# Top-k selection by seven interpolated counts with a branch to a bit search, and the adaLN weight sums on VectorE

## The chip, the cores and the metric

The kernel runs on one core of a Trainium2 chip. A NeuronCore has a matmul engine (TensorE, "PE" in the profile, with its weight loads as "PEld"), and VectorE ("DVE"), ScalarE ("ACT"), GpSimd ("POOL") and SyncE ("SP", which issues the DMAs). Each engine works through its own instructions in order and waits on semaphores for the others. The metric is the device time of one execution in microseconds; the median of several runs is given.

## The reference

A trunk of two layers over 1024 positions and 1024 channels. Each layer modulates its normalised input (adaLN), projects it once, and runs a gated MLP over chunks beside a sparse attention. The attention scores all keys with a small indexer and keeps, for each query, the 256 best:

```python
logits = jnp.einsum('bthd,bsd->bths', qib, k_idx) * (IDX_DIM ** -0.5)
score = jnp.einsum('bth,bths->bts', wb, jax.nn.relu(logits)).astype(jnp.float32)
score = jnp.where(causal[None], score, -jnp.inf)
_, idx = lax.top_k(score, top)                      # top = 256
valid = idx <= qpos[None, :, None]
k_sel, v_sel = gather(k, idx), gather(v, idx)
sc = jnp.einsum('bthd,btkd->bthk', qb, k_sel).astype(jnp.float32) * attn_scale
p = jax.nn.softmax(jnp.where(valid[:, :, None, :], sc, -jnp.inf), axis=-1)
return jnp.einsum('bthk,btkd->bthd', p, v_sel)
```

adaLN: `mod = silu(c) @ w_ada + b_ada`, cut into shift, scale and gate; `h = layer_norm(x) * (1 + scale) + shift`; at the end `x = layer_norm(ALPHA * x + gate * (y @ w_out))`.

## The kernel before

Queries are handled in eight blocks of 128 rows, one query per partition. Block i sees (i + 1) x 128 keys, so blocks 0 and 1 keep every key and only blocks 2 to 7 need a selection. Nothing is gathered: the kernel computes dense attention and adds a mask of 0 or -3e38, so the selection has to deliver, for each row, which 256 keys stay.

A layer (`layer`, L871) goes through these stages:

1. keys, values and indexer queries are projected, then `scores` (L496) builds a float32 tile `sc2` to `sc7` of 128 x (i + 1) x 128 per block: TensorE makes the logits of a head, ScalarE applies the relu, VectorE multiplies by the head's weight and adds up (L513).
2. the remaining input projections (`specs`, L878 to L884): v, q, u, z_a, z_b, two weight slices each, four accumulations of 24 matmuls (L326) into a PSUM accumulator `acc`, of which there are two. `u_za` takes the u accumulations off on VectorE (L469) and the z_a ones on ScalarE and GpSimd (L472, L473); `zb` uses ScalarE alone. The spatial gating (`sgu`, L445) lies between. Between the yields of these projections `side` (L905) advances two kinds of generators: the searches in `gens`, all of them at each step, and the adaLN weight sums in `back`, from the sixth weight slice on. So selection and adaLN sums lie beside the projections in each engine's queue; a scheduler in the compiler then orders each engine's instructions by its own estimate, within stretches that a branch ends.
3. attention per block and half of the heads (`att_soft`, L660, and `att_pv`, L686), interleaved with the output projection (L735), its weights being loaded and multiplied by the gate first (`load_wout`, L710).

The search before is exact, in three groups of blocks (`GROUPS`, L53): blocks 7, 6 and 5 search the 256th largest score bit by bit, the count of each of 31 bits being made on ScalarE (L544) with decisions on VectorE (L545, L553); blocks 4 and 3 search 16-bit keys in two times 16 counts on VectorE (L574, L583, L585); block 2 searches 31 bits with float32 counts on VectorE (L519, L552, L553). A count is one VectorE pass that compares a whole tile with a threshold per row and adds up the hits:

```python
self.nc.vector.tensor_scalar(j[:, :n], sc, thr, None, op0=op, op1=ALU.add, accum_out=out)
```

At the start of attention `select_mask` (L636) turns each tile into its mask: a count, an equality pass, a scan (L647) to cut ties, two more passes (L648, L649) and a GpSimd pass (L650).

`ada_sum` (L166) adds up `w_ada` rows weighted by the condition, over eight slices of 128 x 1024 per sum, three sums in layer 0 (its own gate, and shift and scale of layer 1) and one in layer 1. `ADAE` (L64) chooses the engine: 0 is GpSimd, a multiply (L182) and an add (L184) per slice.

## Time and profile before

| what | us |
|---|---|
| median of 3 runs | 1233.45 (1232.51 to 1239.79) |
| the profiled execution | 1233.29 |
| its span, first to last instruction | 1231.5 |
| TensorE busy | 1119.0 |
| VectorE busy | 977.5 |
| ScalarE busy | 707.1 |
| GpSimd busy | 706.5 |

The profile is of one execution. "Busy" counts an engine's own instructions, not its waits. A view by stretches gives each engine's busy time between two moments of the span; the view in order of time gives start and length of single instructions, and a length can reach into the next instruction, so the distance from start to start is what an instruction costs its engine's queue. A count is followed by a short instruction that reads the accumulator (DVE_READ_ACCUMULATOR).

### The profile page before, as it was taken

To read this page: it belongs to the slowest core of one execution; us is meant where nothing else is said; L and a number is where in the kernel's file an instruction comes from. 1 tells how busy PE (TensorE), PEld (TensorE's weight loads), DVE (VectorE), ACT (ScalarE), POOL (GpSimd) and SP (SyncE) were. 2 spreads that over 40 slices of the span, in tenths; PEclk is the share of its full clock that TensorE was granted. 3 is DMA by queue.
4 is the path that set the end of the run, shared out by engine and by line. 5 is a ranking of instruction groups with operands and counts; after the bars stand their busy time and mean duration, and the time that the engine had idled before them with its cause. 6 is when DMAs were issued, how large, how long until landed. Compare 5 with 4: busy or idle time off the path is not lost.

```text
span 1231.5 us, 18024 instructions
## 1 busy us (share of the span) xinstructions
PE 1119.0 (91%) x5456; PEld 887.3 (72%) x5456; DVE 977.5 (79%) x2776; ACT 707.1 (57%) x1344; POOL 706.5 (57%) x556
## 2 busy tenths in 40 slices
PE   5989999897999499989989999999899967999997
PEld 1568888766788388766667788877678856777885
DVE  6784767998989965788976467599999898878775
ACT  0342655778794164565765345557789535667561
POOL 1574314997794785564765531189633378555753
PEclk9899999998999799999999999999999988999999
DMA  8936332347454474331322463144431434333311
GB/s 257 275 104 165 104 86 79 136 138 222 140 170 154 142 222 125 103 112 44 94 86 69 120 172 86 52 163 137 147 125 52 141 100 142 83 104 86 112 35 60
DMA packets 126777, 152.15 MB, mean 124 GB/s; under 512 B 17108, under 2 KB 94292, under 8 KB 126680
## 3 DMA queue, kind: packets, MB, share of 16 engines
q1 hardware_dynamic: 126680, 151.01, 40.3%
q8 instruction: 43, 0.70, 0.2%
q14 instruction: 54, 0.44, 0.1%
HBM read 111.38 MB, written 35.40 MB: 119 GB/s over the span
## 4 chain that ended last, share of the span: by engine, by line
PE 49%; DVE 30%; issue 7%; ACT 6%; DMA 6%; SPq 2%; POOL 0%; DVEq 0%; ACTq 0%; POOLq 0%
PE pacc L326 18%; PE pacc L735 13%; DVE junkd L574 4%; PE ps L673 4%; PE ppt L693 4%; DVE junkd L519 3%; PE ppt L506 3%; ACT junka L544 3%; PE po L699 2%; PE po L698 2%; PE ps L506 2%; DMA h<-in_w_ada 1%; DVE gb L647 1%; DVE bn L211 1%; DVE bi L553 1%
## 5 line engine op out<-in xcount | busy, mean ns | idle before, releaser
L326 PE MATMUL pacc<-h,w 128*128 128x512 f32 (+2 forms) x2304 | 550.0, 393 | 13.0 <-ACT gc L472 4.8
L326 PEld LDWEIGHTS pacc<-h,w 128*128 128x128 f32 (+1 forms) x2304 | 423.6, 189 | 111.2 <-ACT gc L472 6.4
L280 POOL TENSOR_TENSOR w<-wr,w 128x512 fp32r<-128x512 f32 (+1 forms) x100 | 131.6, 1334 | 168.4 <-ACT w L279 161.2
L544 ACT ACTIVATE junka<-sc,bi 128x1024 int8<-128x1024 f32 x186 | 193.5, 1040 | 51.0 <-DVE bi L553 23.4
L735 PE MATMUL pacc<-h,gc 128*128 128x512 f32 x768 | 196.5, 400 | 2.9 <-ACT gc L279 2.5
L735 PEld LDWEIGHTS pacc<-h,gc 128*128 128x128 f32 x768 | 142.6, 191 | 31.8 <-ACT gc L279 3.2
L513 DVE SCALAR_TENSOR_TENSOR sc<-gc,wi,sc 128x384 f32<-128x384 f32 (+3 forms) x140 | 101.8, 768 | 52.6 <-ACT gc L508 50.1
L673 PE MATMUL ps<-kd,q 128*128 128x512 f32 (+4 forms) x384 | 106.2, 376 | 31.5 <-DVE mx L674 24.8
L697 DVE TENSOR_TENSOR ga<-ppt,ga 128x512 fp32r<-128x512 f32 x144 | 96.6, 684 | 18.1 <-ACT ga L696 17.2
L696 ACT ACTIVATE ga<-ppt 128x512 fp32r<-128x512 f32 x144 | 82.7, 593 | 34.8 <-PE ppt L693 33.6
L574 DVE TENSOR_SCALAR_CACHE_REDUCE junkd<-r,cnt 128x640 bf16<-128x640 int16 (+3 forms) x128 | 102.5, 801 | 0.1
L673 PEld LDWEIGHTS ps<-kd,q 128*128 128x128 f32 x384 | 65.6, 198 | 49.5 <-DVE mx L674 37.1
L682 POOL TENSOR_SCALAR w<-w,rd 128x256 f32<-128x256 f32 (+6 forms) x77 | 62.5, 815 | 42.5 <-DVE rd L681 22.7
L679 ACT ACTIVATE w<-w,mx 128x256 f32<-128x256 f32 (+6 forms) x77 | 60.7, 788 | 42.6 <-DVE mx L674 42.0
L279 ACT ACTIVATE w<-wr 128x512 fp32r<-128x512 f32 (+1 forms) x100 | 56.0, 598 | 44.1 <-DMA wr<-in_w_in 22.0
L693 PE MATMUL ppt<-ident,w 128*128 128x128 f32 x349 | 75.5, 277 | 0.3 <-ACT gc L256 0.3
L216 POOL TENSOR_TENSOR rs<-rs,mhalf 128x1 f32<-128x1 f32 x48 | 32.1, 676 | 73.1 <-DVE rs L215 73.0
L693 PE MATMUL ppt<-ident,ya 128*128 128x128 f32 x227 | 59.1, 277 | 15.4 <-DVE modT L192 15.4
L698 PE MATMUL po<-ga,vv 128*128 128x512 f32 x144 | 62.1, 431 | 9.4 <-DVE gb L705 6.4
L508 ACT ACTIVATE gc<-ppt 128x384 f32<-128x384 f32 (+3 forms) x96 | 47.9, 525 | 36.9 <-PE ppt L506 31.5
L184 POOL TENSOR_TENSOR r<-r,r 128x1024 f32<-128x1024 f32 x28 | 68.2, 2437 | 0.1
L345 POOL TENSOR_TENSOR ga<-ga,ga 128x512 fp32r<-128x512 f32 (+2 forms) x40 | 48.4, 1215 | 33.5 <-ACT ga L344 29.2
(202 smaller groups left out, 2109.4 us busy)
## 6 DMA issues: line engine op xcount, KB each, us to landing
wr<-in_w_in SPq DMA_DIRECT2D x50, 512.0 KB, 4.2
r<-in_w_ada SPq DMA_DIRECT2D x32, 512.0 KB, 4.3
q<-q SPq DMA_DIRECT2D x112, 128.0 KB, 3.0
q<-ga SPq DMA_DIRECT2D x48, 256.0 KB, 2.2
h<-in_w_ada SPq DMA_DIRECT2D x32, 256.0 KB, 5.4
wr<-in_w_out SPq DMA_DIRECT2D x16, 512.0 KB, 4.0
r<-r SPq DMA_DIRECT2D x14, 512.0 KB, 3.4
r<-x SPq DMA_DIRECT2D x12, 512.0 KB, 4.2
```

Of the source, the lines that this page charges most:

```text
L184: eng.tensor_tensor(acc, acc, w, op=ALU.add)
L280: self.nc.gpsimd.tensor_tensor(lo, src, hi.bitcast(F32), op=ALU.subtract)
L326: self.nc.tensor.matmul(acc[:m, :tn], w[:, k, :m], h[:, k % 2, t0:t0 + tn], start=(k == 0 and i == 0), stop=(k == NK - 1 and i == 2))
L513: nc.vector.scalar_tensor_tensor(sc[:, c0:c0 + w], r[:, :w], wsc, sc[:, c0:c0 + w], op0=ALU.mult, op1=ALU.add)
L544: nc.scalar.activation(j[:, :ns[c]], scs[c], AF.Sign, bias=thr, accum_out=cnt[:, c:c + 1])
L574: self.nc.vector.tensor_scalar(j[:, :keys.shape[1]], keys, thr, None, op0=ALU.is_ge, op1=ALU.add, accum_out=out)
L673: nc.tensor.matmul(ps[:, :w], q[:, g * 4 + h, :], self.KD[x][:, c0:c0 + w], start=(x == 0), stop=(x == 1))
L693: nc.tensor.transpose(pt[:, h * P:(h + 1) * P], pr[h][:, kt * P:(kt + 1) * P], self.ident)
L696: nc.scalar.activation(ph, pt, AF.Copy)
L697: nc.vector.tensor_tensor(pl, pt, ph.bitcast(F32), op=ALU.subtract)
L698: nc.tensor.matmul(o, self.V[:, kt, :], ph, start=(kt == 0), stop=False)
L735: self.nc.tensor.matmul(acc, s[:, k, :], m[:, cs], start=(first and k == i == 0), stop=(not more and k == 3 and i == 2))
```

## The change

The selection is rebuilt. Six blocks form two groups, 2 to 4 and 5 to 7. For each row a first threshold comes from mean and variance of its first 256 scores and a table (`start_table`), with a guessed bracket around it. Seven times the threshold is counted; the bracket's lower end (count at least 256) or upper end (count below 256) is replaced by it, and the next threshold is interpolated between the ends for a count of 252. The counts run on VectorE, the arithmetic between them on GpSimd, on 128 x 3 to 128 x 12 elements. A row is left over when the upper end's count is below 248 after seven steps. TensorE adds up the rows left over, VectorE reads the sum into a register, and where it isn't zero a branch runs `exact` for the three blocks of the group: a float32 bit search of 31 bits on VectorE, with scans for ties. Behind the branch each block gets its mask: the keys above the upper end stay, and of the others the up to eight largest are taken with a max-8 and a match-and-replace. All of it now lies beside the projections, and attention starts with finished masks. `side` advances one search per step, in turn, where it advanced all.

With `ADAE = (1, 1, 1)` all adaLN sums run on VectorE, one instruction per slice (a scaled add) instead of GpSimd's two.

The diff, cut to its core:

```diff
-    GROUPS = ((0, 7, 6, 5), (16, 4, 3), (32, 2))
-    MLEAD = 16
+    GROUPS = ((2, 3, 4), (5, 6, 7))
+    STEPS = 7
-    ADAE = (0, 0, 0)
+    ADAE = (1, 1, 1)
...
+    def select(self, masks, blocks, grp):
...
+        yield
+        for k in range(self.STEPS):
+            for c, i in enumerate(blocks):
+                self.count(masks[i], (i + 1) * P, V[:, 0, c:c + 1], ALU.is_ge, C[:, c:c + 1])
+            pool.tensor_scalar(V[:, 1, :], C, 1.0, -float(MID), op0=ALU.mult, op1=ALU.add)
+            pool.tensor_scalar(M[:, 0, :, :], rep(C, 2), float(TOP), 1.0, op0=ALU.is_lt, op1=ALU.mult)
+            pool.tensor_scalar(M[:, 1, :, :], rep(C, 2), float(TOP), 1.0, op0=ALU.is_ge, op1=ALU.mult)
+            pool.tensor_scalar(M[:, 2, :, :], rep(C, 2), float(TOP), 1.0, op0=ALU.is_lt, op1=ALU.mult)
+            pool.tensor_tensor(pair(Z), pair(Z), M[:, 0:2].rearrange("p h k g -> p h (k g)"), op=ALU.mult)
...
+            pool.tensor_tensor(Z, Z, U, op=ALU.add)
...
+            elif k + 1 < self.STEPS:
+                pool.tensor_tensor(W, Z[:, 0:2, :], Z[:, 2:4, :], op=ALU.subtract)
+                pool.tensor_tensor(R, W[:, 1, :], self.minus6[:, :G], op=ALU.pow)
+                pool.tensor_tensor(R, R, W[:, 0, :], op=ALU.mult)
+                pool.tensor_tensor(R, R, Z[:, 1, :], op=ALU.mult)
+                pool.tensor_tensor(V[:, 0, :], Z[:, 0, :], R, op=ALU.subtract)
+            yield
+        bad = small("sb", 1)[:, 0, :]
+        pool.tensor_scalar(bad, Z[:, 3, :], float(TOP - 8 - MID), 1.0, op0=ALU.is_lt, op1=ALU.mult)
+        pt = self.p("pt")
         for c in range(G):
+            nc.tensor.matmul(pt[0:1, 0:1], bad[:, c:c + 1], self.ones[:, 0:1], start=(c == 0), stop=(c + 1 == G))
         yield
+        flag = self.t(f"flag{grp}", [1, 1], I32)
+        nc.vector.tensor_copy(flag, pt[0:1, 0:1])
+        yield
+        v = nc.vector.value_load(flag[0:1, 0:1])
+        with self.tc.If(v != 0):
+            for c, i in enumerate(blocks):
+                self.exact(masks[i], (i + 1) * P)
+                nc.vector.memset(Z[:, 2, c:c + 1], 1.5)
+                nc.vector.memset(Z[:, 3, c:c + 1], float(TOP - 8 - MID))
...
+        for c, i in enumerate(blocks):
+            sc, n = masks[i], (i + 1) * P
+            w = self.g("gb", [P, SEQ], BF16)
+            nc.vector.tensor_scalar(w[:, :n], sc, Z[:, 2, c:c + 1], -2.0 * LOW, op0=ALU.is_lt, op1=ALU.mult)
+            nc.vector.scalar_tensor_tensor(sc, w[:, :n], LOW, sc, op0=ALU.add, op1=ALU.min)
+            yield
+            m8 = self.t("m8", [P, 8], bufs=2)
+            nc.vector.max(m8, sc)
+            nc.vector.tensor_tensor(m8, m8, Q[:, c, :], op=ALU.min)
+            yield
+            nc.vector.match_replace(sc, m8, sc, LOW)
+            nc.vector.tensor_scalar(sc, sc, LOW, NEG, op0=ALU.not_equal, op1=ALU.mult)
+            yield
+
+    def exact(self, sc, n):
...
         for b in range(30, -1, -1):
...
+            cnt, dec, f2 = self.cnt_tile(), self.int_tile(), self.int_tile()
+            self.count(sc, n, f[:, 0:1].bitcast(F32), ALU.is_ge, cnt)
+            nc.vector.tensor_scalar(dec, cnt, float(TOP), float(1 << b), op0=ALU.is_lt, op1=ALU.mult)
+            nc.vector.tensor_scalar(f2, dec, f[:, 0:1], (1 << b) >> 1, op0=ALU.bitwise_xor, op1=ALU.bitwise_xor)
             f = f2
...
-                for g in gens:
-                    next(g, None)
+                while gens and next(gens[0], 0) == 0:
+                    gens.pop(0)
+                gens.append(gens.pop(0)) if gens else None
...
-            for i in order:
-                if i > 1 and t == max(2 * order.index(i) - self.MLEAD, -1):
-                    self.select_mask(masks[i], i)
```

How the order moves, in layer 0. First VectorE, before, where the third u accumulation of the second slice is taken off (`ya` times `pacc`, L469); `junkd` and `cnt` are a count, `bi` the bits of a threshold:

```order
L585 TENSOR_SCALAR cnt_3247<-cnt_3246,cnt_3184 128x1
L519 TENSOR_SCALAR junkd_3258,cnt_3256<-sc_208_1070,bi_3197 128x384
L553 TENSOR_SCALAR bi_3241<-bi_3231,bi_3178 128x1
L585 TENSOR_SCALAR cnt_3247<-cnt_3246,cnt_3184 128x1
L469 TENSOR_TENSOR ya_2001<-ya_2001,pacc_3852 128x512
L552 TENSOR_SCALAR bi_3257<-cnt_3256 128x1
L545 TENSOR_SCALAR bi_3231<-cnt_3230 128x1
L553 TENSOR_SCALAR bi_3260<-bi_3257,bi_3197 128x1
```

And VectorE now, around the u accumulations of that slice (in the new kernel's lines L493): the end of the first branch body (L658 is its last line), two of these products, the second group's flag and its branch:

```order
L656 SCALAR_TENSOR_TENSOR gb_3435<-gb_3434 128x640
L657 SCALAR_TENSOR_TENSOR gb_3435<-gb_3435,gb_3434 128x640
L658 TENSOR_TENSOR sc_247_1183<-gb_3435,gb_3434 128x640
L610 UNCONDITIONAL_BRANCH x2
L493 TENSOR_TENSOR ya_1858<-ya_1858,pacc_4497 128x512
L493 TENSOR_TENSOR ya_1858<-ya_1858,pacc_4535 128x512
L607 CAST flag_572_2648<-ppt_2482 1x1
L609 TENSOR_LOAD flag_572_2648
L610 COMPARE_AND_BRANCH
L544 TENSOR_SCALAR junkd_3458,cnt_3455<-sc_281_1286 128x768
```

Where the products stood between single counts, they now stand behind a whole body, and the next two behind the next.

Then GpSimd at the same place, before: adaLN sums (`r`, L182 and L184), weight splits (`w`, L280) and gating products (`ya`, L473):

```order
L473 TENSOR_TENSOR ya_1636<-ya_1636,gc_3500 128x512
L184 TENSOR_TENSOR r_3816<-r_3816,r_3978 128x1024
L182 TENSOR_SCALAR r_4077<-r_4077,cond_61 128x1024
L473 TENSOR_TENSOR ya_1747<-ya_1747,gc_3566 128x512
L184 TENSOR_TENSOR r_3816<-r_3816,r_4011 128x1024
L280 TENSOR_TENSOR w_3678<-wr_3673,w_3677 128x512
L280 TENSOR_TENSOR w_3678<-wr_3675,w_3677 128x512
L473 TENSOR_TENSOR ya_1747<-ya_1747,gc_3632 128x512
```

And GpSimd now, around its own jump (every engine has one, since a branch ends a stretch of the program; only VectorE decides): `sm`, `ss`, `su`, `sv` and `sc` belong to the second group's search, `sk` and `sq` to the first group's masks:

```order
L304 TENSOR_TENSOR w_4486<-wr_4483,w_4485 128x512
L497 TENSOR_TENSOR ya_1753<-ya_1753,gc_4471 128x512
L579 TENSOR_SCALAR sv_420_1738<-sc_425_1743 128x3
L580 TENSOR_SCALAR sm_424_1742<-sc_425_1743 128x6
L610 UNCONDITIONAL_BRANCH
L581 TENSOR_SCALAR sm_424_1742<-sc_425_1743 128x6
L582 TENSOR_SCALAR sm_424_1742<-sc_425_1743 128x6
L616 TENSOR_SCALAR sk_980_3445<-ss_408_1686 128x3
L583 TENSOR_TENSOR ss_422_1740<-ss_422_1740,sm_424_1742 128x12
L584 TENSOR_TENSOR su_421_1739<-sv_420_1738,sm_424_1742 128x12
L618 TENSOR_SCALAR sq_981_3446<-iota_8_77,sk_980_3445 128x8 x3
L586 TENSOR_TENSOR ss_422_1740<-ss_422_1740,su_421_1739 128x12
```

The adaLN sums are gone from this queue, and the steps of the searches stand in their place, each waiting for counts of VectorE and for one another.

TensorE at the same place, before: the u accumulations of the second slice (`pacc_3689`, `pacc_3757`) follow each other, with a first logit of attention (`ps`, L673) between:

```order
L326 MATMUL pacc_3689<-h_284,w_3397 128x512
L326 MATMUL pacc_3689<-h_280,w_3398 128x512
L673 MATMUL ps_4542<-kd_589,q_4493 128x256
L673 MATMUL ps_4542<-kd_590,q_4493 128x256
L326 MATMUL pacc_3757<-h_505,w_3397 128x512
L326 MATMUL pacc_3757<-h_509,w_3397 128x512
```

And TensorE now: the second of the two u accumulations, `pacc_4535`, ends, the third, `pacc_4573`, begins in the accumulator that `pacc_4497` leaves, and behind its first two matmuls stands the sum of the second group's rows left over (`ppt_2482`, L604):

```order
L350 MATMUL pacc_4535<-h_516,w_4331 128x512
L350 MATMUL pacc_4535<-h_520,w_4331 128x512
L350 MATMUL pacc_4535<-h_516,w_4332 128x512
L350 MATMUL pacc_4573<-h_285,w_4337 128x512
L350 MATMUL pacc_4573<-h_289,w_4337 128x512
L604 MATMUL ppt_2482<-ones_79,sb_547_2480 1x1 x3
L224 MATMUL ppt_4528<-r_4227,ones_79 1x512
L224 MATMUL ppt_4531<-r_4227,ones_79 1x512
L350 MATMUL pacc_4573<-h_285,w_4338 128x512
```

TensorE's jump for the first branch stands 12 matmuls before the end of `pacc_4535`; that for the second 7 matmuls before the end of `pacc_4573`, and the 24 of the fourth, `pacc_4604`, come behind it. In layer 1 both jumps stand 6 matmuls before the end of the third u accumulation of its second slice, and the 24 of the fourth come behind them.

## Rows read from the trace of the kernel before

**Rows 1.** The page of the profile: busy time of each engine, and shares of the chain.
```profile
PE 1119.0 (91%) x5456; PEld 887.3 (72%) x5456; DVE 977.5 (79%) x2776; ACT 707.1 (57%) x1344; POOL 706.5 (57%) x556
...
PE 49%; DVE 30%; issue 7%; ACT 6%; DMA 6%; SPq 2%; POOL 0%; DVEq 0%; ACTq 0%; POOLq 0%
```

**Rows 2.** Busy us (instructions) per engine, TensorE clock, DMA share, GB/s, by stretch.
```profile
207.00:398.00 191.00, 174.81 (x863) 139.91 (x862) 178.06 (x730) 138.99 (x251) 155.25 (x110) 0.96 0.52 162
398.00:425.00 27.00, 14.67 (x76) 12.33 (x74) 26.96 (x27) 7.31 (x9) 18.49 (x10) 0.79 0.32 100
811.00:990.00 179.00, 169.69 (x835) 134.64 (x834) 170.06 (x713) 135.05 (x243) 102.15 (x78) 0.98 0.40 127
990.00:1024.00 34.00, 16.92 (x65) 13.02 (x63) 34.00 (x44) 11.87 (x16) 28.55 (x13) 0.76 0.34 108
```

**Rows 3.** The same for the projection line L326 alone: TensorE, weight loads, clock, DMA.
```profile
207.00:425.00 218.00, 171.11 (x708) 134.45 (x707) 0.94 0.49 154
811.00:1025.00 214.00, 167.78 (x706) 132.86 (x704) 0.94 0.39 124
```

**Rows 4.** TensorE in order of time, 395 to 432 us: start, length, what, [idle before].
```profile
394.73 15.58 PE L326 MATMUL pacc<-h,w 128*128 128x512 f32 x68
...
428.06 0.47 PE L693 MATMUL ppt<-ident,ya 128*128 128x128 f32 x1 [15.39 <-DVE modT L192]
```

**Rows 5.** VectorE in order of time, layer 0: start, length, what.
```profile
337.66 0.87 DVE L574 TENSOR_SCALAR_CACHE_REDUCE junkd<-r,cnt 128x640 bf16<-128x640 uint16 x1
338.45 0.08 DVE L574 DVE_READ_ACCUMULATOR junkd<-r,cnt 128x1 f32 x1
...
339.56 0.60 DVE L519 TENSOR_SCALAR_CACHE_REDUCE junkd<-sc,bi 128x384 int8<-128x384 f32 x1
340.09 0.08 DVE L519 DVE_READ_ACCUMULATOR junkd<-sc,bi 128x1 f32 x1
```

**Rows 6.** VectorE in order of time, layer 1, 968 to 979 us.
```profile
968.89 1.27 DVE L519 TENSOR_SCALAR_CACHE_REDUCE junkd<-sc,bi 128x1024 int8<-128x1024 f32 x1
970.09 0.08 DVE L519 DVE_READ_ACCUMULATOR junkd<-sc,bi 128x1 f32 x1
970.21 1.15 DVE L519 TENSOR_SCALAR_CACHE_REDUCE junkd<-sc,bi 128x896 int8<-128x896 f32 x1
971.28 0.08 DVE L519 DVE_READ_ACCUMULATOR junkd<-sc,bi 128x1 f32 x1
971.39 1.01 DVE L519 TENSOR_SCALAR_CACHE_REDUCE junkd<-sc,bi 128x768 int8<-128x768 f32 x1
972.33 0.08 DVE L519 DVE_READ_ACCUMULATOR junkd<-sc,bi 128x1 f32 x1
972.45 0.17 DVE L566 TENSOR_SCALAR bi<-cnt 128x3 int32<-128x3 f32 x1
...
978.13 0.16 DVE L631 TENSOR_TENSOR bi<-bi,bi 128x2 int32<-128x2 int32 x1
978.33 0.88 DVE L519 TENSOR_SCALAR_CACHE_REDUCE junkd<-sc,bi 128x640 int8<-128x640 f32 x1
```

**Rows 7.** Groups by shape on VectorE: count, busy us, mean ns, idle before.
```profile
L553 DVE TENSOR_SCALAR bi<-bi,bi 128x1 int32<-128x1 int32 x248 | 46.7, 204 | 0.8
...
L552 DVE TENSOR_SCALAR bi<-cnt 128x1 int32<-128x1 f32 x62 | 8.7, 141 | 0.0
```

**Rows 8.** Lines L647 and L648: duration ns min/median/max, first and last start us, forms.
```profile
L647 DVE TENSOR_TENSOR_SCAN gb<-gb x12: 944/1614/2278, 385.1 to 1017.8; 128x384 f16<-128x384 f16 x2, 128x512 f16<-128x512 f16 x2, 128x640 f16<-128x640 f16 x2, 128x768 f16<-128x768 f16 x2
L648 DVE SCALAR_TENSOR_TENSOR gb<-gb,cnt,gb x12: 619/1857/3181, 386.1 to 1020.8; 128x384 f16<-128x384 f16 x2, 128x512 f16<-128x512 f16 x2, 128x640 f16<-128x640 f16 x2, 128x768 f16<-128x768 f16 x2
```

**Rows 9.** GpSimd: the weight split's group (columns of rows 7), and line L216 (of rows 8).
```profile
L280 POOL TENSOR_TENSOR w<-wr,w 128x512 fp32r<-128x512 f32 x90 | 123.7, 1389 | 156.5 <-ACT w L279 155.5 <-PE pacc L326 1.0
L216 POOL TENSOR_TENSOR rs<-rs,mhalf x48: 545/556/1065, 8.1 to 1225.9; 128x1 f32<-128x1 f32 x48
```

**Rows 10.** VectorE line L855, columns of rows 8.
```profile
L855 DVE SCALAR_TENSOR_TENSOR ga<-h,cond,ga x14: 698/750/1759, 18.9 to 44.9; 128x512 f32<-128x512 f32 x14
```

More of the change, by code (lines that the diff above doesn't have):

```diff
@@ L22 @@
 D = 1024
-S = 1024
+S = SEQ = 1024
 DEPTH = 2
@@ L28 @@
 TOP = 256
+MID = 252
+LOW = -2.0 ** 126
 EPS = 1e-5
@@ L47, in two_pi_parts, with start_table @@
     return parts
+def start_table():
+    import numpy as np
+    from statistics import NormalDist
+    nd = NormalDist()
+    tab = np.zeros((P, 6, 6), np.float32)
+    for i in range(2, NB):
+        for p in range(P):
+            n = i * P + p + 1
+            z = nd.inv_cdf(1.0 - (MID + 0.5) / (n + 1))
+            above = lambda y: n * (1.0 - nd.cdf(y)) - MID
+            tab[p, :, i - 2] = (z - 1.2, z, z + 1.2, min(above(z + 1.2), -9.0), above(z - 1.2), 1.0 / (n * nd.pdf(z)))
+    return np.concatenate([tab.reshape(P, 36), np.tile(np.arange(8, dtype=np.float32), (P, 1))], axis=1)
 class Trunk:
@@ L105, in consts @@
         nc.gpsimd.memset(self.mhalf, -0.5)
+        self.half6 = self.col("half6", 1, 6)
+        nc.gpsimd.memset(self.half6, 0.5)
+        self.minus6 = self.col("minus6", 1, 6)
+        nc.gpsimd.memset(self.minus6, -1.0)
+        self.iota8 = self.col("iota8", 1, 8)
+        self.ztab = self.t("ztab", [P, 6, 6])
         self.ones = self.col("ones", 1)
@@ L126, in rope_tables @@
         nc.sync.dma_start(self.invf, a["inv_freq"])
+        nc.sync.dma_start(self.ztab, a["ztab"][:, 0:36].rearrange("p (k g) -> p k g", k=6))
+        nc.sync.dma_start(self.iota8, a["ztab"][:, 36:44])
         pi = self.g("ga", dt=I32)[:, :W]
@@ L494, with scores @@
     SC_R = ('gc',)
-    def scores(self, l, i):
+    def scores(self, l, i, sc):
         nc = self.nc
@@ L521, in int_tile @@
     def int_tile(self):
[L522 removed]
+        return self.col("bi", 8, 1, I32)
     def cnt_tile(self):
[L525 to L570 removed]
@@ L572, in count16 @@
-    def count16(self, keys, thr, out):
-        j = self.t("junkd", [P, 6 * P], BF16)
-        self.nc.vector.tensor_scalar(j[:, :keys.shape[1]], keys, thr, None, op0=ALU.is_ge, op1=ALU.add, accum_out=out)
-    def search16(self, keys, t):
-        nc, G = self.nc, len(keys)
-        for b in range(15, -1, -1):
-            cnt, dec, t2 = (self.cnt_tile() for _ in range(3))
-            for c in range(G):
-                self.count16(keys[c], t[:, c:c + 1], cnt[:, c:c + 1])
-            for c in range(G):
-                nc.vector.tensor_scalar(dec[:, c:c + 1], cnt[:, c:c + 1], float(TOP), -float(1 << b), op0=ALU.is_lt, op1=ALU.mult)
-            for c in range(G):
-                nc.vector.tensor_scalar(t2[:, c:c + 1], dec[:, c:c + 1], t[:, c:c + 1], float((1 << b) >> 1), op0=ALU.add, op1=ALU.add)
-            t = t2
-            yield
-        return t
@@ L636, in select_mask @@
-    def select_mask(self, sc, i):
-        nc = self.nc
-        n = (i + 1) * P
-        thr = self.thr[i]
-        cnt = self.cnt_tile()
-        cge, ceq, room = (cnt[:, k:k + 1] for k in range(3))
-        self.count(sc, n, thr, ALU.is_ge, cge)
-        eq = self.g("gb", [P, S], F16)
-        nc.vector.tensor_scalar(eq[:, :n], sc, thr, None, op0=ALU.is_equal, op1=ALU.add, accum_out=ceq)
-        nc.vector.tensor_scalar(room, ceq, cge, float(TOP), op0=ALU.subtract, op1=ALU.add)
-        pre = self.g("gb", [P, S], F16)
-        nc.vector.tensor_tensor_scan(pre[:, :n], eq[:, :n], eq[:, :n], 0.0, op0=ALU.add, op1=ALU.max)
-        nc.vector.scalar_tensor_tensor(eq[:, :n], pre[:, :n], room, eq[:, :n], op0=ALU.is_gt, op1=ALU.mult)
-        nc.vector.scalar_tensor_tensor(sc, sc, thr, eq[:, :n], op0=ALU.is_lt, op1=ALU.max)
-        nc.gpsimd.tensor_scalar(sc, sc, NEG, 0.0, op0=ALU.mult, op1=ALU.add)
+        return self.col("cnt", 8, 1)
@@ L925, in layer @@
                 for i in range(2, NB):
-                    masks[i] = self.scores(l, i)
-                gens = []
-                for kind, *grp in self.GROUPS:
-                    scs = [masks[i] for i in grp]
-                    gens.append(self.select16(scs, grp) if kind == 16 else self.select(scs, grp, kind == 0))
+                    masks[i] = self.t(f"sc{i}", [P, (i + 1) * P])
+                    self.drain(self.scores(l, i, masks[i]))
+                gens += [self.select(masks, b, k) for k, b in enumerate(self.GROUPS)]
                 self.sgu_setup(l)
@@ L1049 @@
     f = (np.float64(10000.0) ** (-np.arange(0, 64, 2) / 64.0)).astype(np.float32)
-    inputs = dict(inputs, inv_freq=np.tile(f, 4).reshape(P, 1))
-    for name in _INS + ["inv_freq"]:
+    inputs = dict(inputs, inv_freq=np.tile(f, 4).reshape(P, 1), ztab=start_table())
+    for name in _INS + ["inv_freq", "ztab"]:
         arr = np.ascontiguousarray(inputs[name])
```

147 lines of the change are left out of this document (57 added, 90 removed).

## The prediction

> **What bounds the kernel now.** I read the page first [rows 1]: TensorE is busy 91% of the 1231.5 us, VectorE 79%, and the chain that ended last is half TensorE and 30% VectorE. So where VectorE does not feed TensorE in time, the kernel waits. Then I cut out the stage that the change touches, once per layer: from the end of the indexer scores (207 us, 811 us) to the start of attention [rows 2]. In its longer part both engines are nearly full: TensorE 174.8 and VectorE 178.1 of 191 us in layer 0, 169.7 and 170.1 of 179 in layer 1. In its tail VectorE is full (27.0 of 27, 34.0 of 34) and TensorE only half busy: VectorE is building the masks. Then I looked for TensorE's floor: 708 and 706 projection matmuls still lie in this stage [rows 3], and 68 of them in a row take 15.58 us [rows 4], 0.229 us each, or 5.5 us for one accumulation of 24. 708 of them are 162 us. TensorE's other work there is the 18 us by which its busy time in rows 2 (174.8 and 14.7) passes the projections' 171.1 in rows 3; some of it is already attention, and I take 12. That is 174 us of a stage of 218 (207 to 425): at most 44 us can be won, and 39 of the 213 in layer 1. The second row of rows 4 shows where some of it lies: TensorE sits 15.4 us behind VectorE's queue.
>
> **Does the branch run?** No trace can tell, since it hangs on the data, so I worked the seven counts out in float32 on the reference's own inputs. A row is left for the bit search when the last upper threshold counts fewer than 248 keys. Of the 384 rows of a group that leaves 4 and 8 in layer 0 and 6 and 4 in layer 1; one is enough, because the flag is the sum over all rows of three blocks. The cause is in the step: it aims at 252 and keeps only the newest threshold on each side. With 256 keys at one end and 255 at the other it extrapolates past both and can lose a good threshold; one row counts 268, 247, 256, 255, 242, 254, 247. Noise of 1e-5 on the scores moves each group by a row or so, never to zero. So I take all four branch bodies to run.
>
> **The body.** It is VectorE work alone, block after block, every instruction needing the one before. A round is a count, its accumulator read, the decision and the new threshold. From a count to its accumulator read: 0.53 us at 384 keys, 0.79 at 640 [rows 5], 0.94, 1.07 and 1.20 at 768, 896 and 1024 [rows 6]; 512 lies between, 0.66. From that read to an instruction that needs it: 0.12 (972.33 to 972.45, rows 6). A decision lasts 0.14 and a threshold 0.20 [rows 7], and what needs a result starts 0.04 after its end (978.13 + 0.16 to 978.33, rows 6): 0.18 and 0.24. A round is thus its count plus 0.54:
> blocks 2 to 4: 1.98 + 3 x 0.54 = 3.60 us, 32 rounds (a count against zero and 31 bits): 115 us;
> blocks 5 to 7: 3.21 + 1.62 = 4.83 us: 155 us.
> Behind each block come a last count, an equality pass, two scans and four passes over two operands. Scans take 0.94 to 2.28 us and the passes 0.62 at the shortest and up to 3.2 [rows 8], so some 5.4 us at 384 keys and 11.9 at 1024: 20 us and 32 us. The bodies are 135 and 187 us, 322 per layer, 644 in all. Below: if the small instructions overlap as they do between independent blocks (0.21 us issued 0.13 apart, rows 5), a round adds 0.25 and a layer has 266 us. Above: nothing overlaps and the passes run at their slowest, 380 us. I take 322, which rests on dependent pairs of instructions as these are.
>
> Rows 6 show what a count's length costs: each 128 keys more take 0.13 us, float32 in and int8 out. The Trainium skill, "VectorE: DVE Perf Modes", in its perf-mode tier table, has a float32 tensor_scalar in SBUF at two elements per 0.96 GHz cycle, which would be 0.07 us; by that rule a layer's bodies would be some 70 us shorter (an estimate from that page) and the time below 1672 us. The trace does not agree for this form, a count that also accumulates, and its number decides.
>
> **What lies beside it.** Almost nothing. All engines work in order, and a projection has two PSUM accumulators. In layer 0 the order puts the first body before the two products that empty both: TensorE has 12 matmuls left of the second, 3 us, then waits. Between the bodies VectorE does these two products and reads the next flag; in the second body TensorE has 31 matmuls, 7 us. In layer 1 the bodies follow each other and TensorE has 30 matmuls beside them. After the last body some eleven mask passes stand ahead of the next product, 8 us. The flag's way (a matmul, a copy, a load into a register, the compare) has no row; its four steps lie between the 0.12 us of a handover (rows 6) and the 0.55 of the shortest GpSimd arithmetic [rows 9], 0.5 to 2.2 us, and I take 2.
>
> **What goes, and what else comes.** The old counts, on VectorE and on ScalarE, stood beside a TensorE that was nearly full; their going can only free the slack of 44 and 39 us above, and the old masks in the tail are part of that slack. The new start has a chain of its own: seven steps per group, each three counts on VectorE and 7 to 12 small GpSimd instructions that wait for one another. The shortest GpSimd arithmetic in the trace is 0.55 us, for one element, and that is a power (rows 9); a multiply or a compare must be cheaper, and I take 0.3, with 0.55 as the upper end. Some 160 of them before the flag are 48 us; with 15 weight splits of 1.39 us [rows 9], three rotary halves (five such instructions each) and the rest, GpSimd needs about 105 us from the end of the scores to the flag, at the upper end 145. TensorE comes to the flag's matmul after 313 projection matmuls and its 12 us, at 84 us in layer 0, and after 348, at 91, in layer 1. So it waits some 15 to 20 us there. The adaLN sums cost VectorE 32 passes over 1024 columns, from the 512-column row [rows 10] 1.4 to 1.5 us each, 46 us, 35 of them in layer 0; with the early counts (6 x 1.98 + 7 x 3.21 = 34 us) that is 69 of the 105 us before the branch, and the gating norms have the rest. GpSimd's chain hides them; without that cover they would cost up to 20 us. The new masks (six passes per block, some 26 us a layer) lie beside the last twelve accumulations, the two small loads of the table at the start beside the weight loads: nothing.
>
> **The sum.** Layer 0: 105 to the flag, 135 + 187 for the bodies, 4 for products and flags between, 8 of masks, then twelve accumulations (288 matmuls), 66: 505 us against 218, +287. Layer 1: the same terms, 505 against 213, +292. Together +579 on the profiled execution's 1233.3 us (span 1231.5 and 1.8 around it), which is within 0.2 of the median: 1812 us. Low end: bodies of 266 and the flag when TensorE comes (84, 91): 1665. High end: bodies of 380 and a chain of 145: 2008.
>
> **The rivals.**
> *The bodies are jumped over*: faster. For it: a chain of counts that settles is plainly possible, and only about one row in a hundred fails. Against it: 384 rows share a flag. Then the stage is 105 plus what TensorE has left: 395 matmuls, 90 us, and 358, 82 us: 195 and 187 against 218 and 213, 1184 us. It decides once all four groups have no row left over. With the chain at 145 us the same case would end at 1264, with TensorE's own pace at about 1150.
> *Some bodies run*: each one jumped takes 135 or 187 us off, so three of four give 1625 or 1677. For it: the groups with four rows; against it: the noise trial above.
> *The body hides*: VectorE's search lies beside projections as the old one did, and only VectorE's total counts. Then the stage is VectorE's sum: 105 before the branch, 322, and 26 of masks, 453 us against 218 and 213, +475 and 1708 us. The two accumulators speak against it; it lies inside my range.
>
> **How the numbers follow.** All four bodies, as summed or partly hidden: 0.91. Some of them: 0.04. None: 0.05, of which 0.04 faster and the rest with a slow chain. The time is that of the first. Its two ends (1665 and 2008) ask that every doubtful term falls on one side; I take 1670 to 1940. The three runs lie 0.6% apart, so 1% is about what a measurement of this kernel can tell from no change. Faster by over 1%: 0.04; within 1%: 0.01; slower: 0.95.
>
> **What would show it.** Right: in each layer two stretches of some 135 and 187 us in which VectorE runs lines 638 to 658 of the new kernel (counts, decisions, thresholds in turn) with TensorE idle but for a dozen to thirty matmuls; rounds of 1.1 us at 384 keys and 1.7 at 1024; attention that starts with its masks there. Wrong in a term: rounds nearer 0.8 or 1.3 us at 384 keys, or TensorE waiting much more or less than 20 us for the first flag. Wrong altogether: no instruction of lines 638 to 658 in the trace, or TensorE busy beside them.

## The result, and the profile after

The changed kernel takes 1855.41 us (median of 4 runs, 1852.08 to 1857.59) against 1235.09 before: 1.501 times, 95% interval 1.496 to 1.507. Slower was forecast, 1812 us with a range of 1670 to 1940. The profiled execution took 1852.1 us, with a span of 1850.3.

The page after, to be held against [rows 1]: busy time of each engine, two of its lines in 40 slices of the span (tenths busy, and the granted clock of TensorE in tenths), and the chain's shares.

```profile
PE 1125.3 (61%) x5480; PEld 891.7 (48%) x5480; DVE 1434.6 (78%) x3448; ACT 502.3 (27%) x972; POOL 689.2 (37%) x862
...
PE   6899987400300049899989999890000001989998
...
PEclk8899998755655569999999999995555555999999
...
DVE 41%; PE 38%; POOL 7%; issue 6%; DMA 5%; ACT 2%; SPq 1%; DVEq 0%; POOLq 0%; ACTq 0%
```

TensorE's work is the same as before (1125 us against 1119); its share falls from 91% to 61% because of two gaps, one in each layer, which the PE line shows as zeros. Over the zeros the clock stands at half, the lower of its two levels (1.2 GHz).

The stretches after, in the columns of [rows 2]: up to the flag, first body, second body, the last accumulations; layer 0, then layer 1.

```profile
227.00:342.00 115.00, 94.20 (x502) 74.49 (x501) 93.23 (x176) 21.32 (x36) 102.47 (x191) 0.93 0.49 154
343.00:478.00 135.00, 2.19 (x10) 1.49 (x8) 125.18 (x421) 1.15 (x2) 3.67 (x12) 0.52 0.02 6
480.50:665.00 184.50, 14.92 (x58) 10.42 (x56) 174.64 (x420) 1.15 (x2) 2.58 (x6) 0.54 0.01 3
665.00:743.00 78.00, 69.72 (x301) 57.71 (x301) 31.09 (x55) 16.78 (x25) 32.55 (x22) 0.91 0.37 120
1139.00:1239.00 100.00, 91.61 (x522) 72.75 (x520) 71.69 (x160) 20.07 (x35) 88.94 (x199) 1.00 0.29 96
1239.50:1374.20 134.70, 12.23 (x50) 8.81 (x50) 124.88 (x420) 1.15 (x2) 2.04 (x3) 0.56 0.03 8
1374.20:1558.70 184.50, 0.00 (x0) 0.00 (x0) 174.68 (x421) 0.00 (x0) 4.85 (x11) 0.50 0.00 0
1558.70:1636.00 77.30, 68.02 (x288) 56.07 (x289) 32.05 (x55) 16.54 (x25) 23.54 (x15) 0.90 0.37 120
```

The bodies are the second, third, sixth and seventh row, in which VectorE works nearly alone: 134.8 us (342.87 to 477.63) and 184.5 (480.54 to 665.07) in layer 0, 134.7 and 184.5 in layer 1, 638.5 together. TensorE is busy for 29 us of them, ScalarE for at most 1.2 and GpSimd for at most 4.9 us in each, and the DMA share is at most 0.03. TensorE in order of time shows the same gaps from its side, each ended by VectorE; the brackets hold the idle time before the row and its releaser.

```profile
336.94 8.25 PE L350 MATMUL pacc<-h,w 128*128 128x512 f32 x35
478.36 1.22 PE L350 MATMUL pacc<-h,w 128*128 128x512 f32 x2 [133.18 <-DVE ya L493]
...
667.05 1.01 PE L214 MATMUL ppt<-ones,r 128*128 128x1 f32 x4 [171.63 <-DVE r L225]
...
1567.98 68.23 PE L350 MATMUL pacc<-h,w 128*128 128x512 f32 x288 [316.26 <-DVE ya L493]
```

VectorE in order of time answers to [rows 5 to 7]: the flag's copy and the first count of the first body in layer 0, a round at 384 keys, the first instruction behind that body, the ends of the second body, and two counts in a row at 1024 keys in layer 1.

```profile
341.93 0.14 DVE L607 CAST flag<-ppt 1x1 int32<-1x1 f32 x1
342.87 0.55 DVE L544 TENSOR_SCALAR_CACHE_REDUCE junkd<-sc 128x384 int8<-128x384 f32 x1 [0.80 <-DVE flag L607]
...
343.85 0.61 DVE L544 TENSOR_SCALAR_CACHE_REDUCE junkd<-sc,bi 128x384 int8<-128x384 f32 x1
344.38 0.09 DVE L544 DVE_READ_ACCUMULATOR junkd<-sc,bi 128x1 f32 x1
344.50 0.15 DVE L644 TENSOR_SCALAR bi<-cnt 128x1 int32<-128x1 f32 x1
344.69 0.21 DVE L645 TENSOR_SCALAR bi<-bi,bi 128x1 int32<-128x1 int32 x1
344.94 0.61 DVE L544 TENSOR_SCALAR_CACHE_REDUCE junkd<-sc,bi 128x384 int8<-128x384 f32 x1
...
477.63 1.28 DVE L493 TENSOR_TENSOR ya<-ya,pacc 128x512 f32<-128x512 f32 x2
...
480.54 0.95 DVE L544 TENSOR_SCALAR_CACHE_REDUCE junkd<-sc 128x768 int8<-128x768 f32 x1 [0.55 <-DVE flag L607]
...
665.07 1.34 DVE L624 TENSOR_SCALAR gb<-sc,ss 128x384 bf16<-128x384 f32 x3
...
1545.32 1.28 DVE L544 TENSOR_SCALAR_CACHE_REDUCE junkd<-sc,bi 128x1024 int8<-128x1024 f32 x1
...
1547.08 1.28 DVE L544 TENSOR_SCALAR_CACHE_REDUCE junkd<-sc,bi 128x1024 int8<-128x1024 f32 x1
```

A round is 1.09 us at 384 keys (343.85 to 344.94) and 1.76 at 1024 (1545.32 to 1547.08). Of the 1.09, the count takes 0.53; 0.12, 0.19 and 0.25 pass to the decision, the threshold and the next count.

### The profile page after: what moved, and what is told of

It reads as the page before. It is cut to its first block, busy times and chain, and to the rows that moved or that the text cites. A ratio compares the mean times of both kernels' runs of the same rounds, so it can differ in the third digit from the quotient of the medians.

```text
span 1850.3 us, 18487 instructions
## 1 busy us (share of the span) xinstructions
PE 1125.3 (61%) x5480; PEld 891.7 (48%) x5480; DVE 1434.6 (78%) x3448; ACT 502.3 (27%) x972; POOL 689.2 (37%) x862
## 4 chain that ended last, share of the span: by engine, by line
DVE 41%; PE 38%; POOL 7%; issue 6%; DMA 5%; ACT 2%; SPq 1%; DVEq 0%; POOLq 0%; ACTq 0%
DVE junkd L544 21%; PE pacc L350 17%; PE pacc L743 9%; DVE bi L645 4%; DVE bi L644 3%; DMA r<-in_w_ada 3%; PE ps L681 3%; PE ppt L701 3%; POOL w L304 2%; PE po L707 2%; PE po L706 1%; PE ppt L529 1%; DVE gb L656 1%; DVE gb L653 1%; DVE r L200 1%
## 5 line engine op out<-in xcount | busy, mean ns | idle before, releaser
L350 PEld LDWEIGHTS pacc<-h,w 128*128 128x128 f32 (+1 forms) x2304 | 428.9, 191 | 579.4 <-DVE ya L493 476.3
L544 DVE TENSOR_SCALAR_CACHE_REDUCE junkd<-sc,bi 128x512 int8<-128x512 f32 (+5 forms) x384 | 363.0, 945 | 12.9
L496 ACT ACTIVATE gc<-pacc 128x512 f32<-128x512 f32 x16 | 9.4, 590 | 548.5 <-PE pacc L350 548.4
L214 PE MATMUL ppt<-ones,r 128*128 128x1 f32 x32 | 4.4, 250 | 171.6 <-DVE r L225 171.6
L544 DVE TENSOR_SCALAR_CACHE_REDUCE junkd<-sc,sv 128x384 int8<-128x384 f32 (+2 forms) x84 | 79.0, 940 | 26.4 <-POOL sv L598 21.0
L497 POOL TENSOR_TENSOR ya<-ya,gc 128x512 f32<-128x512 f32 x16 | 21.1, 1320 | 204.6 <-ACT gc L496 204.6
L645 DVE TENSOR_SCALAR bi<-bi,bi 128x1 int32<-128x1 int32 x372 | 79.6, 214 | 12.9
L214 PEld LDWEIGHTS ppt<-ones,r 128*128 128x128 f32 x32 | 4.8, 207 | 172.1 <-DVE r L225 171.7
L573 POOL TENSOR_SCALAR ss<-ztab 128x3 f32<-128x3 f32 x8 | 5.1, 661 | 189.1 <-DVE gb L624 187.6
```

Of the source, the lines that this page charges most:

```text
L350: self.nc.tensor.matmul(acc[:m, :tn], w[:, k, :m], h[:, k % 2, t0:t0 + tn], start=(k == 0 and i == 0), stop=(k == NK - 1 and i == 2))
L645: nc.vector.tensor_scalar(f2, dec, f[:, 0:1], (1 << b) >> 1, op0=ALU.bitwise_xor, op1=ALU.bitwise_xor)
```

## The experiments

Theory: the four bodies are the loss, and they run because the interpolation throws good thresholds away. Rivals: the new chain and the moved sums lose by themselves; seven counts are too few; the branch has a price of its own. Every ratio below is against the kernel before, run on the same chip. Three chips were used, and the kernel before took 1237.68, 1237.15 and 1236.42 us on them, so times of different runs can be held against each other to about 1 us, beside the scatter of each run. A pace (`PACE`) is how many steps of the searches are advanced between two pieces of the projections; with it move the counts, the flags and the adaLN sums.

**A flag that is never set.**

```diff
-        pool.tensor_scalar(bad, Z[:, 3, :], float(TOP - 8 - MID), 1.0, op0=ALU.is_lt, op1=ALU.mult)
+        pool.tensor_scalar(bad, Z[:, 3, :], -4096.0, 1.0, op0=ALU.is_lt, op1=ALU.mult)
```

> The changed kernel with a flag that is never set: everything up to the branch and behind it runs, the four bodies are jumped over. Left out: the bit search of the 22 rows that the counts leave over. Theory (the four bodies are the loss): in the changed kernel's trace they last 134.8 + 184.5 us in each layer; 1855 less 638 is 1217; the restart of 9 us behind the bodies goes too (18), TensorE's some 90 matmuls that lay beside the bodies come back (20): 1205 to 1230 us. Rival A (the new chain and the moved sums lose by themselves, without any body): 1240 to 1265. Rival B, the blind price of a jumped body: 1184. TensorE idle for less than 40 us in the stage of layer 0, not 320.

Measured: 1230.21 us, 0.994 (0.992 to 0.996) of the kernel before. So 625 us lay in the bodies and what they leave idle, and without them the kernel is 0.6% faster than before. Both rivals fall, A because this is not slower than before, B (1184) because it is 46 us above it; the next run shows 14 of these.

**No branch at all.** The flag's matmuls, copy, register load, compare and body are cut out.

```diff
-        bad = small("sb", 1)[:, 0, :]
...
-                nc.vector.memset(Z[:, 3, c:c + 1], float(TOP - 8 - MID))
+        yield
+        yield
```

> The same without flag matmuls, flag copy, register load, compare and body at all; the same 22 rows are left out. Theory: the flag's way costs what the trace shows, about 0.5 to 0.9 us in VectorE's queue at each of four places, so at most 4 us below the run with the flag never set. Rival (a conditional region costs on every engine, because each has to jump and to fetch from behind the body): 10 to 30 us below it.

Measured: 1216.44 us, 0.982 (0.980 to 0.985). That is 13.8 us below the run with the flag never set, more than the theory allowed and in the rival's range. That every engine pays, as the rival has it, is not shown; what VectorE pays, its order of time in the run with the flag never set does show (DVEq is its sequencer, L610 the compare and branch):

```profile
339.95 0.14 DVE L607 CAST flag<-ppt 1x1 int32<-1x1 f32 x1
343.74 1.29 DVE L493 TENSOR_TENSOR ya<-ya,pacc 128x512 f32<-128x512 f32 x2 [3.65 <-DVEq L610]
346.41 0.15 DVE L607 CAST flag<-ppt 1x1 int32<-1x1 f32 x1 [1.38 <-PE ppt L604]
349.92 2.40 DVE L624 TENSOR_SCALAR gb<-sc,ss 128x384 bf16<-128x384 f32 x3 [3.36 <-DVEq L610]
...
941.50 1.37 DVE L624 TENSOR_SCALAR gb<-sc,ss 128x384 bf16<-128x384 f32 x3 [7.07 <-DVEq L610]
```

A branch that jumps over its body leaves VectorE idle for 3.4 to 3.7 us, and in layer 1 7.1 for two in a row; together 14.1, about what the kernel gains without them. In the changed kernel, where the branch falls into the body, the next count started 0.94 us after the flag's copy (341.93 to 342.87, above), idle for 0.80 of it. The register load of the flag is in both (0.55 and 0.56 us at these two places) and so is the compare (0.07); behind the compare 2.9 us are left with the jump. So it is the jump that costs, not the flag.

**A short jump.** One round in each body, flag never set.

```diff
-        for b in range(30, -1, -1):
+        for b in range(0, -1, -1):
```

> The run with the flag never set, with one round of the bit search in each body in place of 31, so that the jump is over some 40 instructions of VectorE per block fewer than a hundred, not over 310 per body. Left out: the bit search of the 22 rows, as there. Theory (the 3.4 to 3.7 us behind a jumped branch is the way to far code): the gap falls below 1.5 us and the time by 6 to 12 us, near the run with no branch (1216). Rival (any taken jump costs this, however short): gaps of 3 us or more and 1227 to 1235.

Measured: 1220.46 us, 0.988 (0.984 to 0.992), 9.8 below the long jump, as the theory has it. VectorE at the same places:

```profile
339.27 0.14 DVE L607 CAST flag<-ppt 1x1 int32<-1x1 f32 x1
340.78 0.69 DVE L493 TENSOR_TENSOR ya<-ya,pacc 128x512 f32<-128x512 f32 x1 [1.37 <-DVEq L610]
...
343.61 0.15 DVE L607 CAST flag<-ppt 1x1 int32<-1x1 f32 x1
344.52 0.97 DVE L624 TENSOR_SCALAR gb<-sc,ss 128x384 bf16<-128x384 f32 x2 [0.76 <-DVEq L610]
...
924.66 2.00 DVE L624 TENSOR_SCALAR gb<-sc,ss 128x384 bf16<-128x384 f32 x3 [1.80 <-DVEq L610]
```

The gaps are 1.37 and 0.76 us, and 1.80 for the two of layer 1: 3.9 in place of 14.1, a difference of 10.2 where the kernel gained 9.8. So the price hangs on the length of the body that is jumped. The Trainium skill, "Runtime: NRT & Kernel Launch", section on instruction fetch mechanics, says that a taken branch to a target outside the fetched window has to wait for that code to be fetched. Both runs agree with it; what the fetch itself took, no trace here shows apart.

**Good thresholds are kept.** A row whose upper end already counts 248 or more keeps that end.

```diff
         for k in range(self.STEPS):
...
+            if k:
+                pool.tensor_scalar(R, Z[:, 3, :], float(TOP - 8 - MID), float(SEQ), op0=ALU.is_ge, op1=ALU.mult)
+                pool.tensor_tensor(C, C, R, op=ALU.add)
             pool.tensor_scalar(V[:, 1, :], C, 1.0, -float(MID), op0=ALU.mult, op1=ALU.add)
```

> The changed kernel, branch and all, in which a row whose upper count is already 248 to 255 keeps that threshold (two small GpSimd instructions more per step). Nothing is left out. Theory (the branch runs because the step throws good thresholds away, not because seven counts are too few): no row is left over in any group, the bodies are jumped over, and the time is that of the run with the flag never set plus 0 to 8 us (2 x 6 x 2 instructions of 0.2 to 0.28 us a layer on GpSimd): 1205 to 1235. Rival (seven counts are too few for about one row in a hundred): some groups still branch, 135 or 185 us each, 1340 to 1855.

Measured: 1232.84 us, 0.997 (0.995 to 0.999). No bit search stands in its trace; all four branches jump. With two instructions more in six of the seven steps no flag is set, where the float32 working counted 22 rows left over, and the counts are seven as before: the step's rule was the cause, not the number of counts.

**Five counts.**

```diff
-    STEPS = 7
+    STEPS = 5
```

> The same with 5 counts in place of 7. Nothing is left out. By the arithmetic in float32 no row is left over after 5 counts. If GpSimd's chain sets when TensorE goes on: two steps of two groups less, some 12 instructions of 0.28 us each, 13 us a layer, of which VectorE's waits give back 5 to 20 us in all against the run with 7. If TensorE's own matmuls set it: within 5 us of that run. If 5 counts leave a row over: 135 us or more above it.

Measured: 1310.17 us, 1.057 (1.054 to 1.060). None of the three cases: no body runs, and still it is 77 us above the run with 7 counts, 36 of them by the last projection of layer 0 (465.6 in place of 430.0 us) and all by that of layer 1 (1095.5 in place of 1018.3). In order of time on TensorE both flags of a layer stand behind 768 of its projection matmuls now, where they stood behind 923 and 958 in layer 0 and behind 917 and 955 in layer 1, and that gave the next theory.

> The run with 5 counts, with a pace of 0.8 in place of 1.1, which puts the flags of layer 0 behind 825 and 858 projection matmuls of the program in place of 768 and 768. Nothing is left out. Theory (the 77 us that the run with 5 counts lost against 7 come from where its flags stand: both ahead of the gating norms' last products, with TensorE, ScalarE and GpSimd out of work while VectorE goes over the masks): 1215 to 1240, as with 7 counts or a little less. Rival (5 counts cost this in themselves, for instance in a body that runs): 1300 or more.

```diff
-    PACE = 1.1
+    PACE = 0.8
```

Measured: 1233.25 us, 0.998 (0.995 to 1.000). The 77 us are gone with the other pace, which moved the flags of both layers (to 825 and 858, 800 and 833) and the counts with them. The same 55 us around the flags of layer 0, in the columns of [rows 2], first of the run with 5 counts, then of the one with the other pace:

```profile
300.00:355.00 55.00, 18.91 (x129) 13.75 (x130) 40.28 (x97) 0.00 (x0) 20.50 (x65) 0.60 0.11 33
```

```profile
300.00:355.00 55.00, 47.43 (x212) 36.24 (x213) 36.35 (x71) 8.79 (x14) 39.72 (x86) 0.94 0.27 78
```

With the flag too early TensorE, ScalarE and GpSimd have run out of work ahead of it (TensorE 18.9 of 55 us, ScalarE none), and what would feed them stands behind the branch. In both layers together TensorE waits 32.7 us for the sum of the rows left over (5.6 with seven counts) and 30.5 for the gating's norms, and in layer 1, too, it has no projection for 52 us (931.6 to 984.0). Two counts fewer, at the other pace, are worth nothing (1233.25 against 1232.84).

**The adaLN sums, each way.** First back on GpSimd, with good thresholds kept; then the kernel before with nothing but the move to VectorE.

```diff
-    ADAE = (1, 1, 1)
+    ADAE = (0, 0, 0)
```

> The run that keeps good thresholds, with the adaLN weight sums back on GpSimd. Nothing is left out. There each of the 32 takes 1.14 us for the product (L182 of the kernel before) and some 2.4 us for the sum, 3.5 us, 24 of them in layer 0: 85 us in front of and between GpSimd's small instructions. Theory (the move to VectorE is what makes room for the chain): the flag of layer 0 comes 40 to 85 us later or the sums come late, 1255 to 1320. Rival (the sums are in VectorE's way, where TensorE waits 16 to 22 us for the gated products behind them): 5 to 20 us faster than 1232.8.

Measured: 1239.60 us, 1.002 (0.9995 to 1.004), 6.8 above the same kernel with the sums on VectorE: between theory and rival. The flag of layer 0 does come 53 us later (its copy at 403.2 in place of 349.8), but TensorE has projections to do until then, and in the whole run it waits for the gated products of L493 only 6.4 us in place of 16.3.

```diff
-    ADAE = (0, 0, 0)
+    ADAE = (1, 1, 1)
```

> The kernel before with only the adaLN sums moved to VectorE. Nothing is left out. VectorE is busy 178 of 191 us in the stage there, and 32 sums at 1.5 us are 48 us, 36 in layer 0. Theory (VectorE sets the time of that stage before the change, so the move alone costs what it adds): slower by 20 to 48 us. Rival (GpSimd's load was in the way there, with waits of 15 us behind the shift sums): same or up to 15 us faster.

Measured: 1271.62 us, 1.029 (1.025 to 1.034): 34 us, as the theory has it. The move costs beside the old search, which fills VectorE (busy 178 of 191 us of that stage, [rows 2]), and is worth some 7 us, by the two intervals 3 to 10, beside the new one, which leaves VectorE busy for 68% of the span in place of 79%.

**The bit search round by round over three blocks**, with the branch as in the changed kernel.

```diff
         for b in range(30, -1, -1):
...
+            for c, (sc, n) in enumerate(work):
+                self.count(sc, n, f[c][:, 0:1].bitcast(F32), ALU.is_ge, cnt[c])
+            for c in R3:
+                nc.vector.tensor_scalar(dec[c], cnt[c], float(TOP), float(1 << b), op0=ALU.is_lt, op1=ALU.mult)
+            for c in R3:
+                nc.vector.tensor_scalar(f2[c], dec[c], f[c][:, 0:1], (1 << b) >> 1, op0=ALU.bitwise_xor, op1=ALU.bitwise_xor)
```

> The changed kernel with the branch as it is, its bit search written round by round over the three blocks of a group (three counts, three decisions, three thresholds) in place of block after block. Nothing is left out. In the changed kernel a round is its count plus 0.54 to 0.56 us, 1.09 at 384 keys and 1.76 at 1024. Theory (of these 0.55 us half is the wait of an instruction for the one before; between independent blocks a round adds 0.25, the blind lower bound): 32 rounds of 6 blocks save 0.29 us each, 56 us a layer: 1720 to 1765, bodies of some 106 and 157 us. Rival (VectorE takes that time for every instruction, whether it depends or not): within 15 us of 1855.

Measured: 1756.02 us, 1.418 (1.413 to 1.424): 99 below the changed kernel, the theory. One round of the first three blocks:

```profile
363.03 0.60 DVE L544 TENSOR_SCALAR_CACHE_REDUCE junkd<-sc,bi 128x384 int8<-128x384 f32 x1
...
365.27 0.27 DVE L649 TENSOR_SCALAR bi<-cnt 128x1 int32<-128x1 f32 x2
365.46 0.45 DVE L651 TENSOR_SCALAR bi<-bi,bi 128x1 int32<-128x1 int32 x3
365.82 0.60 DVE L544 TENSOR_SCALAR_CACHE_REDUCE junkd<-sc,bi 128x384 int8<-128x384 f32 x1
```

Three thresholds take 0.45 us together here; alone each took 0.21 and stood 0.25 ahead of the next count. The round lasts 2.79 us. The changed kernel's, block after block, sum to 3.69: 1.09, 1.23 at 512 keys and 1.37 at 640. So about half of the 0.55 us beside a count is the wait of an instruction for the one before it. The bodies last 108.5 and 158.3 us in place of 134.8 and 184.5. That way of writing it is the cheaper body, and it still costs 520 us over the kernel before.

**One group of six blocks**, good thresholds kept: one chain, one flag, one jump per layer.

```diff
-    GROUPS = ((2, 3, 4), (5, 6, 7))
+    GROUPS = ((2, 3, 4, 5, 6, 7),)
-    PACE = 1.1
+    PACE = 0.6
```

> The run that keeps good thresholds, with all six blocks in one group: one chain, one flag and one branch per layer in place of two, and a pace of 0.6 in place of 1.1, which puts the flag behind 437 projection matmuls of the layer's stage. Nothing is left out. In the run with the flag never set VectorE stood 3.65 us behind the first jumped branch of layer 0 and 7.07 us behind the two of layer 1, some 3.5 us each. Theory (a jumped branch costs VectorE 3.5 us on the path): two fewer, 7 us, and half the small instructions on GpSimd: 1217 to 1227 against that run's 1232.8. Rival (one chain of six counts and 14 small instructions per step cannot overlap itself, so TensorE waits for it): TensorE waits over 20 us at the flag in each layer, 1250 or more.

Measured: 1213.54 us, 0.984 (0.978 to 0.989), 19.3 below the two groups, more than the 7 that the jumps were to give. There are fewer of them, but each goes over a body of six blocks:

```profile
363.21 0.15 DVE L610 CAST flag<-ppt 1x1 int32<-1x1 f32 x1 [6.88 <-PE ppt L607]
369.13 1.31 DVE L627 TENSOR_SCALAR gb<-sc,ss 128x384 bf16<-128x384 f32 x3 [5.78 <-DVEq L613]
```

5.8 us here and 3.4 in layer 1, 9.2 together, against 5.3, 3.4 and 3.7 in the run with two groups (the fourth lies under another wait). The longer body is not dearer as a rule: in the next run, with six blocks too, the two gaps are 3.8 and 3.6. What made one jump of these two runs take 5.3 and 5.8 stays open. More shows in what TensorE waits for: the gated products of L493 8.6 us in place of 16.3, the sum of the rows left over nothing in place of 5.6, split weights 10.4 in place of 14.5. How much of that is the one chain, and how much the other pace with its later flag, was not tried apart.

```diff
-    STEPS = 7
+    STEPS = 6
-    PACE = 0.6
+    PACE = 0.5
```

> One group of six blocks and good thresholds kept, with 6 counts in place of 7 and a pace of 0.5: the flag of layer 0 behind 962 projection matmuls in place of 1018. Nothing is left out. The chain is 9 us a layer shorter (six counts of 5.2 us and some 14 small instructions of 0.28). Theory (that chain has ended before TensorE comes to the flag, so its length is worth nothing): within 6 us of the run with 7 counts, 1208 to 1220. Rival (it sets the time): 12 to 18 us faster, 1196 to 1202.

Measured: 1215.93 us, 0.982 (0.978 to 0.985): the same as with seven counts within the scatter of the runs, as the theory has it. At its pace the shorter chain is worth nothing. One group with good thresholds kept is under both kernels: 1.6% (1.1 to 2.2) below the kernel before, with the branch and its bit search still in place for inputs that need them.

## Why the prediction was right, and where it was off

**Four bodies run, and nothing hides them**: right. The jumped rival had the right sign and the wrong price, 1184 against 1230.21, because the flag's way, taken as 2 us with an upper bound of 2.2, fits a branch that falls through (0.7 to 0.95 us) and not a jump over the body, 3.4 to 3.7, four times; and the rival's sum held no such term at all. By the trace of the run with the flag never set the rest lies elsewhere: the stage of layer 0 lasted 221 us (207 to 427.7) against the rival's 195, where 7 us more are the jumps and 15 the later end of the scores, as below; that of layer 1 187 against 187; and the rest of the span was 25 us more than I counted, as in the sum below.

**The body's size**: right, which is the reason why the time is. 135 and 187 were forecast, 134.8 and 184.5 came; the rounds of 1.07 and 1.74 (a count plus 0.54) came as 1.09 and 1.76. The mean round is 1.09 at 384 keys and 1.79 at 1024, so over 32 rounds the forecast is some 7 us a layer too low, while the passes behind the blocks, 20 and 32 forecast, came to some 16 and 27; so the sum is nearer than its parts, by luck. Reading the price of a dependent pair off two handovers in [rows 6] was the step that carried this, and the run round by round shows that the choice mattered: the lower bound, 266 a layer for instructions that overlap, is what that run reached (108.5 and 158.3: 266.8). The count of 640 keys was read from a search with 16-bit keys (0.79, [rows 5]); the float32 count took 0.81. The counts grew by 0.13 us per 128 keys, as in [rows 6] (612 ns at 384, 1278 at 1024, means of 64). So the rate in the Trainium skill, "VectorE: DVE Perf Modes", perf-mode tier table, by which the prediction's estimate was a time below 1672, does not fit this form.

**What lies beside a body**: TensorE had 10, 58, 50 and no matmuls beside the four (10, 46, 48 and none of projections), where I had 12 and 31 in layer 0 and 30 in layer 1. It changes little: TensorE then waits 133, 172 and 316 us.

**Before the flag**: this is the term that was mis-sized. 105 us from the end of the scores were forecast for each layer. Layer 1 took 100 (1138.6 to 1238.9, the flag's copy). Layer 0 took 135 from the 207 us at which the sum starts: its scores ended at 226.8, 17 us later than in the kernel before (209.8), and 115 us followed. Some 13 of the 17 lie ahead of the scores: VectorE's first product of them starts at 137.6 us in place of 124.9, behind 341 projection matmuls in place of 311, which is 7 us of it. In all runs with the new selection it starts between 136 and 140. The sum put nothing there; what brings the rest was not looked for. What TensorE and VectorE waited for in the 115 us, by line, with total, times and longest:

```profile
PE pacc L350 <- DVE ya L493: 14.1, 3, 5.7
PE pacc L350 <- DVE junkd L544: 2.7, 1, 2.7
PE ppt L475 <- DVE gc L244: 1.5, 2, 1.0
...
DVE junkd L544 <- POOL sv L598: 7.5, 4, 3.7
...
DVE r L200 <- DMA r<-in_w_ada: 4.4, 4, 3.3
```

I had let it run through to the flag's matmul, 84 us after the start, and wait 15 to 20 us there; by the prediction's own sign that term is wrong. TensorE came to it 110 us after the scores (336.72) and did not wait, since GpSimd's last instruction before the flag ended at the same time, 110 us in place of the 105 forecast. It had waited 14 us earlier, at its two accumulators (up to 309.5 us): the gated products that empty them stand in VectorE's queue behind counts and adaLN sums, and sums waited 4.4 us for their weights there. The counts' waits for GpSimd, 7.5 us, come after that, and TensorE runs on meanwhile. The groups by shape, over the whole kernel, show the price of the small instructions (columns of [rows 7]):

```profile
L200 DVE SCALAR_TENSOR_TENSOR r<-r,cond,r 128x1024 f32<-128x1024 f32 x28 | 43.0, 1536 | 25.8 <-DMA r<-in_w_ada 25.7
...
L595 POOL TENSOR_TENSOR sr<-sw,minus 128x3 f32<-128x3 f32 x20 | 17.4, 869 | 1.0
...
L596 POOL TENSOR_TENSOR sr<-sr,sw 128x3 f32<-128x3 f32 x20 | 4.8, 239 | 1.0
```

A sum costs VectorE 1.54 us (1.4 to 1.5 forecast), a small multiply on GpSimd 0.24 (0.3 forecast), and the power 0.87, above the 0.55 that [rows 9] show for one element and that I had made the upper end.

**Behind the bodies**: right within 4 us: TensorE went on 9.2 us after the last body (8), and the twelve accumulations, with the new masks beside them, took 68.5 and 68.1 us (66).

**The sum.** Stage of layer 0, 207 to 743: 536 us against 505, +31. Layer 1, 1138.6 to 1636.0: 497.4, −7.6. The rest of the span came out 16.4 us longer than before: 39.8 in all, 1852.1 against 1812.3. One reason is where I ended the stage of the kernel before, at 425 and 1024 [rows 2]: its attention starts on TensorE at 411.62 and 1006.91, so 13 and 17 us in which attention had begun were counted to the stage that the new one replaced. That makes 30 us; so what lies outside the stages has itself become some 14 us shorter, for which I have no row. From last projection to last projection there is nothing of the kind: +333 us to that of layer 0 (410 to 743), +296 from there to that of layer 1 (1007 to 1636), −10 behind it.

**The masks and the sums cost nothing**: not shown apart. Beside the accumulations the masks cost at most the 2 to 3 us by which these came out above the forecast, the sums are a gain beside the new search (6.8 us, the run with them back on GpSimd), and by the run with no branch, 1216 us, the new selection with everything but the bit search is 1.8% faster than the old one.

## What to carry to other kernels

A rare branch on a flag over hundreds of rows is not rare: price its body as if it ran, work out on real data whether it does, and look at the rule that decides before adding steps, since here two small instructions that keep a good threshold saved more than 600 us. A branch that is jumped still left its engine idle for 2.4 to 5.8 us here, with a long body, and it cuts the order of the work, so what feeds the other engines has to stand ahead of it. Between a search over several blocks one after the other and one that goes round over all of them, the second saves half of what lies between the counts.
